# Second half of a hybrid diffusion layer: SyncE's transfers in written order, convolution blocks spread evenly, four output tiles

## The chip, the cores and the metric

The kernel runs on one core of a Trainium2 chip. The metric is the device time of one launch in microseconds (us), the median of several runs; lower is better.

A core has engines with an instruction stream each: TensorE (PE in the profile, with its weight loads as PEld), VectorE (DVE), ScalarE (ACT), GpSimd (POOL) and SyncE (SP). SyncE and ScalarE issue transfers between HBM and the on-chip memory SBUF; each issues them in the order of its own stream, so a transfer whose wait isn't over holds everything behind it on that engine. Matmul results go to PSUM, which has eight banks here.

## The reference

One layer of a backbone with two groups of heads. The context has 256 tokens, the latent grid 2048 tokens in 32 rows of 64. The input projection, shortened:

```python
def trunk_layer(x, mod, grid, h0, ...):
    h = rms_norm(x, g_pre) * (1 + scale) + shift
    u = h @ w_in
    z, xbc, dt_raw, ga, gb, gsil = jnp.split(u, ...)
    y_ssd, h_fin = ssd_branch(z, xbc, dt_raw, ...)
    y_conf = conformer_branch(ga, gb, ...)          # on the grid
    y_conf = y_conf.reshape(...) * jax.nn.silu(gsil)
    out = jnp.concatenate([y_ssd, y_conf], axis=-1) @ w_out
    return x + gate * rms_norm(out, g_post), h_fin

def conformer_branch(ga, gb, conv_w, conv_b, ln_g, ln_b):
    h = ga * jax.nn.sigmoid(gb)
    h = depthwise_conv(h, conv_w, conv_b)           # 31 taps down the columns
    return jax.nn.silu(layer_norm(h, ln_g, ln_b))
```

`ssd_branch` is a two-way Mamba-2 scan in chunks of 128 tokens: inside a chunk, products with a matrix of decays; between chunks, a state of 128 × 64 for each of 16 heads, forward and backward.

## The kernel before

The 2304 tokens (18 tiles of 128: two of context, sixteen of the latent grid) are worked in two halves, tiles 0 to 9 and 10 to 17. Within a half, the projection runs channel block by channel block: a unit takes a weight block of 1024 × 128, split into a high and a low part (wh, wl), and makes for each token block one PSUM group of 24 matmuls (lines 461 to 463). `gab_unit` makes two groups for a token block, gb and ga, gates them (line 625) and stores the result in GL[j] (line 626); `silu_unit` makes the z and gate blocks (store in line 639). wh and wl have three buffers each and are loaded by `load_w` (lines 418 and 419); a unit's load waits until the buffer of the unit three before it is free.

The stretch that the change touches is the second half behind its xbc blocks. There 21 units (eight of ga and gb, eight of z, five of the gate) make up `blocks`, a generator of steps of three matmuls, of which 392 are taken in this stretch. Between these steps run, as generators that are advanced a step at a time:

- the scan over tiles 9 to 17 (`scan`, `pass_a`), a new tile every seven steps. A tile loads xT and bc (lines 733 and 735), transposes them on TensorE (lines 778 and 855), loads rows of decays lb on ScalarE's queue (line 746), masks them on GpSimd (758), exponentiates them on ScalarE (766), mixes them on VectorE (770, 771), multiplies (802, 809, 815 to 817), copies the backward state out (sb, line 831, stored in 832) and sums the output tile yg (838 to 845, stored in 846). The tile yg starts with a skip term (838), which VectorE makes from xT.
- the convolution of the latent grid, eight blocks of 128 channels (`lat_conv`). A block loads kernels kd and image cx (`lat_load`, lines 698 and 699), copies the kernels into order (kt, 707), does 1024 small matmuls into four PSUM banks cp, two by two (718), evacuates each on VectorE into cvv (722), and stores cvv in four transfers (727). kd and cx have two buffers, kt and cvv one. A block asks for the next one's load when its GL is ready.
- the convolution of the context, four blocks on VectorE (`ctx_conv`), whose steps lie between the latent blocks.

PSUM has three banks "mm" for the projection and five banks "ss". A tile's px, pb, py, po and pst and a block's cp all come from the five.

What sets the order: a framework builds every engine's stream by a scheduler that uses its own estimates of durations, and keeps the dependences. An engine wrapped in the class `InOrder` keeps the written order while its flag `on` is set (line 81 is then the profile's line for what it issues). Before, the flag of SyncE is set at the start of the kernel and not here.

The loop of the stretch, before:

```python
extra = chain(f for j in range(4) for f in (lat(2 * j), ctx_conv(j + 4, cg), lat(2 * j + 1)))
sc_ = scan(range(9, NT))
run(take(blocks, 24))
interleave(take(blocks, 24), [sc_] * 4, 24)
interleave(take(blocks, 344), merge(sc_, 63, extra, 8 * 6 + 4 * 13), 344)
```

`merge` distributes the 100 steps of `extra` evenly among 63 of the scan.

Of the kernel before, what the change touches and what calls it, by code (L numbers as in the profile page):

```python
# [8 lines left out]
F32 = mybir.dt.float32  # L9
# [8 lines left out]
P = 128  # L18
# [30 lines left out]
def merge(a, na, b, nb):  # L49

    steps, x, y = [], 0, 0
    for _ in range(na + nb):
        if y * na >= x * nb and x < na or y >= nb:
            steps.append(a)
            x += 1
        else:
            steps.append(b)
            y += 1
    return steps


def take(gen, n):
    for _ in range(n):
        yield next(gen, None)
# [20 lines left out]
def backbone_kernel(ctx, tc, xa, xt_in, cols, rows, wconv, conf_b, gp_row, bg_row, state0, w_mod, w_dt, w_in, w_out,  # L85
# [3 lines left out]
    V, S, T, DMA = (InOrder(tc, e) for e in (nc.vector, nc.scalar, nc.tensor, nc.sync))  # L89
# [30 lines left out]
    def place(i):  # L120

        return (0, i) if i < HT[0] else (1, i - HT[0])
# [66 lines left out]
    pa = ph_a.enter_context(tc.tile_pool(name="pa", bufs=1))  # L189
# [423 lines left out]
    def gab_unit(half, j, hb):  # L613
        wb = next_w()
        wa = next_w()
        gl_done.discard(j)
        for b in ORDER[half]:
            BN, o = BNS[b], TOK[b]
            pg = bank("mm", f"gb{half}_{j}_{b}")
            yield from mm_cm(pg, wb, hb[b])  # L620
            th = ev(f"gth{half}_{j}_{b}")[:, :BN]
            S.activation(th, pg[:, :BN], AF.Tanh, scale=0.5)
            pa_ = bank("mm", f"ga{half}_{j}_{b}")
            yield from mm_cm(pa_, wa, hb[b])
            V.scalar_tensor_tensor(th, th, 1.0, pa_[:, :BN], ADD, MUL)
            DMA.dma_start(GL[j][:, o:o + BN], th)
        if half:
            gl_done.add(j)

    def silu_unit(half, c0, dst, j, hb, order=None):  # L630
        w = next_w()
        for b in order or ORDER[half]:
            BN, o = BNS[b], TOK[b] - half * HT[0] * P
            ps = bank("mm", f"sp{half}_{c0}_{j}_{b}")
            yield from mm_cm(ps, w, hb[b])
            th = ev(f"sth{half}_{c0}_{j}_{b}")[:, :BN]
            S.activation(th, ps[:, :BN], AF.Tanh, scale=0.5)  # L637
            V.scalar_tensor_tensor(th, th, 1.0, ps[:, :BN], ADD, MUL)  # L638
            DMA.dma_start(dst[half][j * P:(j + 1) * P, o:o + BN], th)


    def gate_rows():
        acc = [slab(f"gacc{a}") for a in range(2)]
        for k in range(KT):
            wg = big(f"wg{k}")
            DMA.dma_start(wg, w_mod[k * P:(k + 1) * P, 2 * D:3 * D])
            for a in range(2):
                if k == 0:
                    V.here("tensor_scalar", acc[a][:, :D], wg, sc[:, a, 0:1], None, MUL)
                else:  # L650
                    V.here("scalar_tensor_tensor", acc[a][:, :D], wg, sc[:, a, k:k + 1], acc[a][:, :D], MUL, ADD)
            yield
        br = [slab("bgr0")[0:1, :D], slab("bgr1")[0:1, :D]]
        DMA.dma_start(br[0], bg_row)
        DMA.dma_start(br[1], gp_row)
        for a in range(2):
            for n in range(2):
                ps = bank("ss", f"gp{a}{n}")
                cs = slice(n * 512, (n + 1) * 512)
                T.matmul(ps[0:1, :], ones[:, 0:1], acc[a][:, cs], start=True, stop=True)  # L660
                o = big(f"gr{a}{n}")[0:1, :512]
                V.tensor_tensor(o, ps[0:1, :], br[0][:, cs], ADD)
                V.tensor_tensor(o, o, br[1][:, cs], MUL)
                DMA.dma_start(GGD[a:a + 1, cs], o)
        yield


    def ctx_conv(j, tile):
        g = tile(f"cg{j}")
        G.memset(g[:, 0:15], 0.0)  # L670
        G.memset(g[:, 271:286], 0.0)
        DMA.dma_start(g[:, 15:271], GL[j][:, 0:256])
        yield
        acc = g[:, 512:768]
        w0 = C_CONFW + j * CW
        V.here("tensor_scalar", acc, g[:, 0:256], cv[:, w0:w0 + 1], cfb2[:, j:j + 1], MUL, ADD)
        for t in range(1, CW):
            V.here("scalar_tensor_tensor", acc, g[:, t:t + 256], cv[:, w0 + t:w0 + t + 1], acc, MUL, ADD)
            if t % 3 == 0:
                yield  # L680
        o = g[:, 768:1024]
        S.mul(o, acc, 0.5)
        DMA.dma_start(CV[j * P:(j + 1) * P, 0:256], o)
        yield
# [6 lines left out]
    def lat_load(j, lp):  # L691
        kd = lp.tile([P, 32, 32], F32, tag="kd", name=f"kd{j}", bufs=2)
        x = lp.tile([P, 32, 64], F32, tag="cx", name=f"cx{j}", bufs=2)
        lat_in[j] = kd, x
        for a in range(4):
            rs = slice(a * 32, (a + 1) * 32)
            src = bass.AP(tensor=wconv.tensor, offset=(j * 4 + a) * 64 * 32, ap=[[32, 32], [1, 1024]])
            DMA.dma_start(kd[rs].rearrange("p r g -> p (r g)"), src)
            DMA.dma_start(x[rs], GL[j][:, 256:].rearrange("(g a) (r w) -> a r g w", a=4, w=64)[a])

    def lat_conv(j, lp, cbb, more):
# [28 lines left out]
    def pass_a(i):  # L730
        half, il = place(i)
# [102 lines left out]
        yg = {}  # L834

        def skip(g):
            yg[g] = pa.tile([P, 4, P], F32, tag="yg", name=f"yg{i}{g}", bufs=2)
            V.tensor_tensor(yg[g], xT[:, 4 * g:4 * g + 4, :],
                            cv[:, C_D + 4 * g:C_D + 4 * g + 4].unsqueeze(2).to_broadcast([P, 4, P]), MUL)

# [77 lines left out]
    def scan(tiles):  # L918

        gens = [pass_a(i) for i in tiles]  # L920
        live, t = [], 0
        while gens or live:
            if gens and t % 7 == 0:
                live.append(gens.pop(0))
            for g in list(live):
                if next(g, 0) == 0:
                    live.remove(g)
            t += 1
            yield


    def interleave(blocks, side, n):
        done = 0
        total = len(side)
        for a, _ in enumerate(blocks):
            want = min(total, -(-total * (a + 1) // n))
            while done < want:
                next(side[done], None)
                done += 1
        while done < total:  # L940
            next(side[done], None)
            done += 1

    def chain(gens):
        for g in gens:
            yield from g

    def run(gen):
        for _ in gen:
            pass  # L950

    def post(half, nb):
        return chain([gab_unit(half, j, hb) for j in range(8)] + [silu_unit(half, Z0, ZS, j, hb) for j in range(8)]
                     + [silu_unit(half, GS0, GS, j, hb) for j in range(nb)])
# [76 lines left out]
    extra = chain([gate_rows()] + [ctx_conv(j, big) for j in range(4)])  # L1031
# [21 lines left out]
    lp = ph_l.enter_context(tc.tile_pool(name="lp", bufs=1, side="right"))  # L1053
# [4 lines left out]
    blocks = post(1, 5)  # L1058
    cg = lambda name: lp.tile([P, D], F32, tag="cg", name=name, bufs=2)
    lat = lambda j: lat_conv(j, lp, cbb, gl_done.__contains__)  # L1060
    extra = chain(f for j in range(4) for f in (lat(2 * j), ctx_conv(j + 4, cg), lat(2 * j + 1)))
    sc_ = scan(range(9, NT))
    run(take(blocks, 24))
    interleave(take(blocks, 24), [sc_] * 4, 24)
    interleave(take(blocks, 344), merge(sc_, 63, extra, 8 * 6 + 4 * 13), 344)
    run(sc_)
    run(extra)
    ph_l.close()
    ph_a.close()

# [105 lines left out]
    def norms(i, yz, nq):  # L1176

        pm = bank("ss", f"pm{i}")
        src = [(c, e, t[1]) for c, e, t in ((0, 4.0 * EPS, yz), (1, EPS, nq)) if t]
        for c, e, t in src:  # L1180
            T.matmul(pm[:, c:c + 1], t, ones[:, 0:1], start=True, stop=True)
        rs = []
        for c, e, t in src:
            ms = p1.tile([P, 1], F32, tag=f"ms{c}", name=f"yms{i}{c}", bufs=2)
            V.tensor_scalar(ms, pm[:, c:c + 1], 1.0 / D, e, MUL, ADD)
            rs.append((c, rstd_of(p1, ms, f"yr{i}{c}")))
        return rs
# [116 lines left out]
    i = order[0]  # L1304
# [21 lines left out]
    for b in range(2):  # L1326
        for m, u in enumerate(last):
            run(take(u, 8))
            if b == 0 and m == 1:
                rs = norms(i, yz, None)  # L1330
# [18 lines left out]
            if b == 1 and m == 0:  # L1349
                rs = norms(i, None, nq)  # L1350
                nq = conf_sqsum(i1, vv[1][0])
            if b == 1 and m == 1:
                n, v = nn[0], vv[0][0]
# [3 lines left out]
            if b == 1 and m == 2:  # L1357
                gs0, v0, n = gs_load(i), v, nn[1]
# [17 lines left out]
    i, nxt, nx2 = order[:3]  # L1376
    banks(i)
    out_part(pso[i], yh, 0, 1)
    rs = norms(nxt, yz, nq)
# [42 lines left out]
    n, n2 = n2, conf_load(order[3])  # L1422
    yh = yhn

    for a, i in enumerate(order[1:], 1):
# [7 lines left out]
        rs = None if last else norms(nxt, yz, nq)  # L1433
# [46 lines left out]
        if a + 3 < NT:  # L1480
            ssd_load(order[a + 3])
            n, n2 = n2, conf_load(order[a + 3])
        else:
            n = n2
# [72 lines left out]
```

## Time and profile before

| | us |
|---|---|
| median of three runs | 1852.8 |
| least, most | 1851.51, 1853.14 |
| the profiled execution, its own time | 1855.05 |
| its span, first to last instruction | 1853.3 |

The profile is one execution. Its busy times are shares of the span; a row of waits is read "engine, line, waits for", then the total in us, how often, and the longest. "SPq" is SyncE's queue as it issues a transfer. A row of windows holds a stretch, its length, the busy time (and instruction count) of each engine in it, the granted clock of TensorE as a part of full speed, and the transfers' share and rate. A time on a row of issues ("to landing") runs from the issue to the arrival of the data. The rows that matter are in the prediction.

### The profile page before, as it was taken

How to read it: one execution, taken by the hardware profiler on the slowest of the kernel's cores; microseconds unless marked ns; L12 is line 12 of the kernel's file. 1: busy time of each engine (PE TensorE's matmuls, PEld its weight loads, DVE VectorE, ACT ScalarE, POOL GpSimd, SP SyncE). 2: the span in 40 equal slices, each digit the busy share in tenths (PEclk: the TensorE clock that was granted, in tenths of full speed). 3: DMA queues.
4: the chain of work that ended last, by engine and by line, in shares of the span. 5: the costliest groups of instructions: out<-in, count | busy, mean ns of one | idle time of the engine just before them, and what ended most of it. 6: DMA issues, size and time to landing. Idle time of an engine off the chain costs nothing.

```text
span 1853.3 us, 29884 instructions
## 1 busy us (share of the span) xinstructions
PE 1793.9 (97%) x11167; PEld 1480.5 (80%) x11167; DVE 1216.5 (66%) x1847; ACT 867.1 (47%) x1960; POOL 172.2 (9%) x281
## 2 busy tenths in 40 slices
PE   5999999999999999999999889999999999999998
PEld 2888887888888888888877667777787888888886
DVE  4597857575666762687457375868347878777763
ACT  4747424444455431744235344554245545454441
POOL 1002001011111000100002011110000101111110
PEclk9999999999999999999999889999999999999999
DMA  9656566554786654545697889694977666656632
GB/s 334 215 198 238 204 212 212 190 201 162 261 267 216 222 182 145 178 170 201 195 207 225 176 239 233 229 236 176 290 223 238 194 184 167 172 171 170 185 103 80
DMA packets 304429, 375.22 MB, mean 202 GB/s; under 512 B 84246, under 2 KB 203670, under 8 KB 304284
## 3 DMA queue, kind: packets, MB, share of 16 engines
q1 hardware_dynamic: 283548, 335.56, 58.1%
q10 hardware_dynamic: 20736, 37.76, 7.3%
q8 instruction: 88, 1.44, 0.3%
q14 instruction: 57, 0.47, 0.1%
HBM read 243.66 MB, written 129.59 MB: 201 GB/s over the span
## 4 chain that ended last, share of the span: by engine, by line
PE 87%; DMA 8%; issue 1%; ACT 1%; DVE 1%; SPq 1%; POOL 0%; ACTq 0%; POOLq 0%; DVEq 0%
PE op L81 21%; PE sp L461 6%; PE sp L462 6%; PE sp L463 6%; PE xp L462 5%; PE xp L461 5%; PE xp L463 5%; PE ga L461 3%; PE ga L463 3%; PE ga L462 3%; PE gb L461 3%; PE gb L463 3%; PE gb L462 3%; DMA lb<-lt 3%; PE py L802 2%; PE po L809 2%
## 5 line engine op out<-in xcount | busy, mean ns | idle before, releaser
L766 ACT ACTIVATE lb<-lb,WB 128x128 f32<-128x128 f32 x576 | 184.5, 391 | 162.7 <-POOL lb L758 156.6
L461 PE MATMUL sp<-hh,wh 128*128 128x512 f32 (+1 forms) x640 | 240.0, 375 | 0.0
L463 PE MATMUL sp<-hh,wl 128*128 128x512 f32 (+1 forms) x640 | 237.1, 371 | 0.0
L462 PE MATMUL sp<-hl,wh 128*128 128x512 f32 (+1 forms) x640 | 237.0, 370 | 0.0
L758 POOL TENSOR_SCALAR_AFFINE_SELECT lb<-lb 128x512 f32<-128x512 f32 x144 | 109.1, 761 | 729.9 <-ACT el L755 400.5
L463 PE MATMUL xp<-hh,wl 128*128 128x512 f32 (+1 forms) x456 | 168.0, 368 | 0.0
L462 PE MATMUL xp<-hl,wh 128*128 128x512 f32 (+1 forms) x456 | 167.8, 368 | 0.0
L461 PE MATMUL xp<-hh,wh 128*128 128x512 f32 (+1 forms) x456 | 167.0, 367 | 0.0
L558 DVE SCALAR_TENSOR_TENSOR cva<-raw,cwh,cva 128x1280 f32<-128x1280 f32 (+1 forms) x96 | 141.9, 1487 | 20.4 <-ACT cva L552 18.2
L463 PEld LDWEIGHTS sp<-hh,wl 128*128 128x128 f32 x640 | 121.3, 189 | 21.1
L461 PEld LDWEIGHTS sp<-hh,wh 128*128 128x128 f32 x640 | 121.6, 190 | 20.7 <-issue 0.2
L462 PEld LDWEIGHTS sp<-hl,wh 128*128 128x128 f32 x640 | 121.6, 190 | 20.0
L461 PE MATMUL ga<-hh,wh 128*128 128x512 f32 (+1 forms) x320 | 121.3, 379 | 6.4 <-DMA wh<-whd 5.5
L75 DVE SCALAR_TENSOR_TENSOR cg<-cg,cv 128x256 f32<-128x256 f32 x240 | 123.0, 512 | 3.3
L461 PE MATMUL gb<-hh,wh 128*128 128x512 f32 (+1 forms) x320 | 120.5, 376 | 0.0
L463 PE MATMUL ga<-hh,wl 128*128 128x512 f32 (+1 forms) x320 | 119.2, 373 | 0.5 <-DMA wl<-wld 0.5
L462 PE MATMUL ga<-hl,wh 128*128 128x512 f32 (+1 forms) x320 | 119.4, 373 | 0.0
L463 PE MATMUL gb<-hh,wl 128*128 128x512 f32 (+1 forms) x320 | 119.0, 372 | 0.0
L462 PE MATMUL gb<-hl,wh 128*128 128x512 f32 (+1 forms) x320 | 118.9, 371 | 0.0
L770 DVE TENSOR_TENSOR lb<-lb,lb 128x512 f32<-128x512 f32 x72 | 50.8, 706 | 90.0 <-ACT lb L766 71.7
L638 DVE SCALAR_TENSOR_TENSOR sth<-sth,sp 128x512 f32<-128x512 f32 (+1 forms) x80 | 50.4, 630 | 75.6 <-ACT sth L637 70.7
L755 ACT ACTIVATE el<-lb 64x256 f32<-64x256 f32 x136 | 56.3, 414 | 88.8 <-DMA lb<-lt 71.2
(273 smaller groups left out, 3832.9 us busy)
## 6 DMA issues: line engine op xcount, KB each, us to landing
lb<-lt ACTq DMA_DIRECT2D x144, 256.0 KB, 4.6
wr<-in_w_in SPq DMA_DIRECT2D x88, 256.0 KB, 4.9
whd<-wh SPq DMA_DIRECT2D x44, 512.0 KB, 3.4
wld<-wl SPq DMA_DIRECT2D x44, 512.0 KB, 5.2
wh<-whd SPq DMA_DIRECT2D x44, 512.0 KB, 5.5
wl<-wld SPq DMA_DIRECT2D x44, 512.0 KB, 5.9
xT<-xb SPq DMA_DIRECT2D x18, 512.0 KB, 4.2
yp<-yg SPq DMA_DIRECT2D x36, 256.0 KB, 4.9
```

What stands on the lines that cost most here:

```text
L75: return self._tc.keep_in_program_order(getattr(self._eng, name)(*a, **k))
L81: return lambda *a, **k: self._tc.keep_in_program_order(f(*a, **k))
L461: T.matmul(ps[:, :BN], wh[:, k, :], hh[:, k, :], start=(k == 0), stop=False)
L462: T.matmul(ps[:, :BN], wh[:, k, :], hl[:, k, :], start=False, stop=False)
L463: T.matmul(ps[:, :BN], wl[:, k, :], hh[:, k, :], start=False, stop=(k == KT - 1))
L558: V.scalar_tensor_tensor(a[:, :n], raw[:, t:t + n], cwh[:, ct * 5 + t:ct * 5 + t + 1], a[:, :n], MUL, ADD)
L638: V.scalar_tensor_tensor(th, th, 1.0, ps[:, :BN], ADD, MUL)
L755: S.activation(el[g][rs, q:q + 2, :], E[g, hq, 0][rs, j::2, :], AF.Exp)
L758: G.affine_select(E[g, hq, d], E[g, hq, d], pattern=[[0, 4], [sg, P]], compare_op=ALU.is_ge, fill=NEG, base=0, channel_multiplier=-sg)
L766: S.activation(lb[:, h, :], lb[:, h, :], AF.Exp, bias=WB[:, i, c + h:c + h + 1])
L770: V.tensor_tensor(a, a, E[g, hq, 1], ADD)
L802: T.matmul(py[g][j * HD:(j + 1) * HD, q * P:(q + 1) * P], xt[g][:, h * HD:(h + 1) * HD], E[g, hq, 0][:, t, :], start=True, stop=True)
```

## The change

Four things change, all in the second half.

1. `lat_load` brings kd in one transfer of 128 × 1024 (512 KB), before four of 32 × 1024 (128 KB each). The four of cx stay.
2. The output tile yg has four buffers, in another pool, in the second half; before, two.
3. The convolutions: the first block's load is a step of its own at the start; then, for each j, seven steps of a context block, a latent block, the other six steps, a latent block. So the latent blocks are evenly spaced, and each asks for the next one's load early. `extra` has 101 steps.
4. SyncE keeps the written order for the stretch (`DMA.on = True`).

```diff
@@ -692,10 +692,10 @@
         kd = lp.tile([P, 32, 32], F32, tag="kd", name=f"kd{j}", bufs=2)
         x = lp.tile([P, 32, 64], F32, tag="cx", name=f"cx{j}", bufs=2)
         lat_in[j] = kd, x
+        src = bass.AP(tensor=wconv.tensor, offset=j * 4 * 64 * 32, ap=[[64 * 32, 4], [32, 32], [1, 1024]])
+        DMA.dma_start(kd.rearrange("p r g -> p (r g)"), src)
         for a in range(4):
             rs = slice(a * 32, (a + 1) * 32)
-            src = bass.AP(tensor=wconv.tensor, offset=(j * 4 + a) * 64 * 32, ap=[[32, 32], [1, 1024]])
-            DMA.dma_start(kd[rs].rearrange("p r g -> p (r g)"), src)
             DMA.dma_start(x[rs], GL[j][:, 256:].rearrange("(g a) (r w) -> a r g w", a=4, w=64)[a])
@@ -834,7 +834,8 @@
         def skip(g):
-            yg[g] = pa.tile([P, 4, P], F32, tag="yg", name=f"yg{i}{g}", bufs=2)
+            pool, n = (lp, 4) if half else (pa, 2)
+            yg[g] = pool.tile([P, 4, P], F32, tag="yg", name=f"yg{i}{g}", bufs=n)
@@ -948,6 +949,10 @@
+    def run_once(f):
+        f()
+        yield
@@ -1058,13 +1063,17 @@
     lat = lambda j: lat_conv(j, lp, cbb, gl_done.__contains__)
-    extra = chain(f for j in range(4) for f in (lat(2 * j), ctx_conv(j + 4, cg), lat(2 * j + 1)))
+    ctxs = [ctx_conv(j + 4, cg) for j in range(4)]
+    extra = chain([run_once(lambda: lat_load(0, lp))]
+                  + [f for j in range(4) for f in (take(ctxs[j], 7), lat(2 * j), take(ctxs[j], 6), lat(2 * j + 1))])
     sc_ = scan(range(9, NT))
+    DMA.on = True
     run(take(blocks, 24))
     interleave(take(blocks, 24), [sc_] * 4, 24)
-    interleave(take(blocks, 344), merge(sc_, 63, extra, 8 * 6 + 4 * 13), 344)
+    interleave(take(blocks, 344), merge(sc_, 63, extra, 1 + 8 * 6 + 4 * 13), 344)
     run(sc_)
     run(extra)
+    DMA.on = False
```

Two places in the order of the instructions show what moves. The first is on SyncE, around the weight wh3232, that of the ga block of the sixth channel block (names: kd and cx are the convolution's loads, cv its stores, yp and st the scan's stores, gl the gated results, bc and xT a tile's loads). Before:

```order
L698 DMA kd4_10488<-in_wconv 32x1024 x3
L699 DMA cx3_9706<-gl3_71 32x32x64 x4
L846 DMA yp11_90<-yg110_9630 128x512
L832 DMA st11_108<-sb110_9965 128x512
L626 DMA gl4_72<-gth1_4_3_9718 128x512
L698 DMA kd5_10795<-in_wconv 32x1024
L727 DMA cv_78<-cvv2_9760 32x32x64 x4
L698 DMA kd5_10795<-in_wconv 32x1024
L735 DMA bc13_10312<-xb1_64 128x4x128
L698 DMA kd5_10795<-in_wconv 32x1024 x2
L418 DMA wh3232_1_9646<-whd17_137 128x1024
L419 DMA wl3232_1_9645<-wld17_181 128x1024
```

Now:

```order
L81 DMA kd2_9438<-in_wconv 128x1x1024
L81 DMA cx2_9439<-gl2_70 32x32x64 x4
L81 DMA gl3_71<-gth1_3_4_9427 128x512
L81 DMA wh4256_1_9567<-whd25_145 128x1024
L81 DMA wl4256_1_9566<-wld25_189 128x1024
L81 DMA wh3232_1_9571<-whd17_137 128x1024
L81 DMA wl3232_1_9570<-wld17_181 128x1024
L81 DMA cv_78<-cvv1_9451 32x32x64 x4
L81 DMA cg5_9739<-gl5_73 128x256
L81 DMA xT12_9779<-xb1_64 128x8x128
L81 DMA bc12_9781<-xb1_64 128x4x128
L81 DMA gl4_72<-gth1_4_3_9693 128x512
```

The weight stood behind stores of the convolution and parts of kd4 and kd5, two blocks of the convolution ahead of their turn. It now stands directly behind the pair wh4256 and wl4256, and the tile loads xT12 and bc12 stand behind it, four stores and a context load.

The second place is on ScalarE, around the copy of tile 9's second backward state, sb91 (lb are rows of decays: L746 loads one, L766 exponentiates it; the first digits after lb are the tile). Before:

```order
L746 DMA lb10100_9051<-lt1_116 128x512
L766 ACTIVATE lb10010_8985<-lb10010_8985,WB_257 128x128 x4
L746 DMA lb11011_9392<-lt1_116 128x512
L746 DMA lb10110_9113<-lt1_116 128x512
L831 COPY sb91_9016<-pst911_8959 128x512
L864 CAST bth10_9022<-pb10_8967 128x256
L782 COPY xt100_9028<-px100_8972 128x512
L866 COPY cb10_9024<-pb10_8967 128x256
L755 ACTIVATE el101_8880<-lb10100_9051 64x256 x2
L792 CAST xwh1000_9086<-xw1000_9085 128x512
L766 ACTIVATE lb10100_9051<-lb10100_9051,WB_257 128x128 x4
L782 COPY xt101_9093<-px101_9038 128x512
```

Now:

```order
L746 DMA lb10110_9042<-lt1_116 128x512
L766 ACTIVATE lb11001_9314<-lb11001_9314,WB_257 128x128 x4
L766 ACTIVATE lb11011_9374<-lb11011_9374,WB_257 128x128 x2
L755 ACTIVATE el101_8754<-lb10110_9042 64x256 x2
L766 ACTIVATE lb11011_9374<-lb11011_9374,WB_257 128x128 x2
L746 DMA lb11101_9425<-lt1_116 128x512
L766 ACTIVATE lb10110_9042<-lb10110_9042,WB_257 128x128 x4
L766 ACTIVATE lb11101_9425<-lb11101_9425,WB_257 128x128 x4
L746 DMA lb11111_9554<-lt1_116 128x512
L622 ACTIVATE gth1_2_4_9046<-gb1_2_4_8881 128x512
L766 ACTIVATE lb11111_9554<-lb11111_9554,WB_257 128x128 x4
L831 COPY sb91_8888<-pst911_8834 128x512
```

The copy sb91 stood directly behind the loads of lb11011 and lb10110 and ahead of their exponentials. It now stands behind the exponentials of both and of lb11101 and lb11111, whose loads are issued between. The same holds for sb101, sb111 and sb131; each of the four frees the PSUM bank that the second matmul group of a convolution block takes next (blocks 0, 1, 2 and 4).

## The prediction

> **What bounds the kernel now.** I read the page's totals first, then a table by stage, then the waits of TensorE in the stretch that the change touches, then the chain of waits there. The totals say that TensorE is the bound: it is busy for nearly the whole span.
>
> ```profile
> span 1853.3 us, 29884 instructions
> ## 1 busy us (share of the span) xinstructions
> PE 1793.9 (97%) x11167; PEld 1480.5 (80%) x11167; DVE 1216.5 (66%) x1847; ACT 867.1 (47%) x1960; POOL 172.2 (9%) x281
> ```
>
> So the change can win only where TensorE (PE) stands still or runs slowly. The table by stage (length, then busy time and instruction count of PE, PEld, DVE, ACT and POOL, then the granted clock, the DMA share and GB/s) shows where that is: ahead of the scan, with the scan and the convolutions beside the weight groups, and behind them.
>
> ```profile
> 880.00:950.00 70.00, 69.49 (x569) 56.84 (x568) 33.55 (x41) 20.03 (x29) 1.09 (x5) 1.00 0.72 192
> 950.00:1300.00 350.00, 324.12 (x3314) 255.56 (x3314) 237.61 (x408) 165.65 (x415) 44.84 (x63) 0.95 0.80 216
> 1300.00:1420.00 120.00, 118.12 (x570) 98.31 (x567) 59.75 (x82) 47.73 (x89) 2.69 (x4) 1.00 0.81 258
> ```
>
> From 950 to 1300 us PE is idle for 350 − 324.12 = 25.9 us, and the clock is 0.95 where it is 1.00 on either side. That is the whole field of this change. PE's waits between 950 and 1420 us name the 25.9 us almost completely (columns: total, times, longest):
>
> ```profile
> PE ga L461 <- DMA wh<-whd: 5.5, 1, 5.5
> PE px L778 <- issue: 5.3, 2, 4.1
> PE cp L718 <- DVE cvv L722: 4.4, 1, 4.4
> PE pst L815 <- DVE cvv L722: 3.5, 1, 3.5
> PE cp L718 <- issue: 2.6, 1, 2.6
> PE pst L815 <- ACT xwh L792: 1.7, 1, 1.7
> PE cp L718 <- ACT sb L831: 1.4, 1, 1.4
> ...
> PE ga L463 <- DMA wl<-wld: 0.5, 1, 0.5
> ```
>
> These eight sum to 24.9 us. Three kinds matter: a weight that came late (5.5 + 0.5), the PSUM banks of the latent convolution that other engines had not emptied (4.4, 3.5, 2.6 and 1.4), and a tile's transposes that could not start (5.3).
>
> **The change part by part.** *The late weight: −6.0 us.* The chain of waits shows its origin: SyncE's queue (SPq) works through the stores of cvv (L727) and the parts of kd (L698) before it gets to the weight.
>
> ```profile
> 1054.16 0.56 SPq L727
> 1054.78 2.80 SPq L727
> 1057.62 1.51 SPq L727
> 1059.17 1.82 SPq L698
> 1061.52 0.50 SPq L698
> 1063.04 9.06 DMA wl<-wld
> ```
>
> The waits of SPq and the issues of kd say how long the queue had stood there, and what a kd part costs to issue (least, median and most, in ns):
>
> ```profile
> SPq L698 <- ACT kt L707: 24.2, 2, 14.7
> ```
>
> ```profile
> L698 SPq DMA_DIRECT2D kd<-in_wconv x32: 311/421/3385, 910.6 to 1159.7; - x32
> ```
>
> A kd part waits until the copy kt of two blocks before has freed its buffer, and wh3232 and wl3232 stand behind four such parts. In the changed order these two stand directly behind wh4256 and wl4256, and no kd is between. So both stalls of ga go, 5.5 + 0.5 = 6.0 us. The merge of four kd parts into one takes 32 − 8 = 24 issues off SPq, 24 × 0.421 = 10.1 us of queue over 350; apart from the stall just counted, no wait of PE names kd, so I give it nothing more (bounds: none to the 6.0 again, if the order alone had not been enough).
>
> *The blocks spread evenly: −5.8 us of old stalls.* cvv has one buffer. Blocks 1 and 2 of the convolution lie close together in the trace, and the 4.4 us come where the evacuation of block 2 waits for block 1's stores. Blocks one output channel tile apart have time for that, so 4.4 goes; so does the 1.4, whose place no longer exists. Bound: they stay, 0.
>
> *The banks, new stalls: +15.6 us.* This is the dearest term and the least certain. A block takes four of five "ss" banks, and a bank is free when the scan's use of it is evacuated. In the changed order blocks 0, 1, 2 and 4 get their second bank from a state copy sb (L831) on ScalarE, and that copy stands behind the exponentials of about three decay rows lb more than before. What a decay row costs is in the trace: mask, one exponential, and what ended POOL's and DVE's idle time ahead of lb.
>
> ```profile
> L758 POOL TENSOR_SCALAR_AFFINE_SELECT lb<-lb x59: 632/637/1806, 952.4 to 1272.7; 128x512 f32<-128x512 f32 x59
> L766 ACT ACTIVATE lb<-lb,WB x236: 377/387/406, 953.1 to 1274.7; 128x128 f32<-128x128 f32 x118
> ...
>   DMA lb<-lt: 149.5, 38
> ```
>
> A row is 4 × 0.387 = 1.5 us of ScalarE when its data is there, and an engine that waited for one stood 149.5 / 38 = 3.9 us. The sb copy used to be ahead of three such waits. Least is the 1.4 us that the trace shows for PE behind sb; most is three whole waits, 11.8 us. I take one wait, 3.9 us, since the two conv stalls that come from other evacuations (4.4 and 3.5) are of that size: 4 × 3.9 = 15.6. Bounds: 4 × 1.4 = 5.6 to 4 × 11.8 = 47.2, of which the upper would need PE to arrive early at all four.
>
> *The evacuations on VectorE: +3.5 us.* In blocks 5 and 6 the first bank is emptied by VectorE behind the mixing of lb16000 and lb17000. I price each by the 3.5 us of the row "pst <- cvv"; one such stall is there already, so the net is 3.5. Bounds 0 and 2 × 4.4 − 3.5 = 5.3.
>
> *The tile loads: +4.1 us.* In written order xT12 and bc12 stand behind wh3232 and wl3232, four stores of cvv1 and the load of cg5; each of these waits for somebody, and what is queued behind bc12 is the next gated result and the stores of tile 11. The transposes of tile 12 are what waits. The price is the longer wait of the row "px <- issue", 4.1 us, once. Bounds: 0, if the load was asked for early enough, and eight tiles at 4.1 (the second rival). The first weights of the stage, wh3744 and wl3744, now stand behind three stores of xb1 and four loads of cbb; PE shows no wait there in the trace, so I take 0, with 5.5 (the longest weight wait) as the other end.
>
> *yg with four buffers: 0.* VectorE's waits show what it removes:
>
> ```profile
> DVE yg L838 <- DMA yp<-yg: 10.6, 4, 4.2
> ```
>
> None of PE's rows names yg; the mix and the evacuation of cvv, which do stand behind it on VectorE, waited last for decay rows. Bounds: −3.5 (the "pst <- cvv" row, if the 4.2 us ahead of it had been its cause) to 0. The cover is that late decay row; were it early, the four buffers would be worth the 3.5.
>
> *The clock: +3.6 us.* Slices of 10 us in and behind stalls show what a stop costs afterwards:
>
> ```profile
> 1060.00:1070.00 10.00, 5.03 (x23) 3.81 (x21) 5.40 (x11) 4.82 (x12) 0.64 (x1) 0.91 0.91 241
> 1070.00:1080.00 10.00, 9.04 (x39) 6.75 (x40) 6.37 (x13) 4.61 (x12) 1.27 (x2) 0.75 0.82 280
> ...
> 1220.00:1230.00 10.00, 10.00 (x248) 7.75 (x250) 5.80 (x10) 4.40 (x13) 0.75 (x2) 1.00 1.04 292
> 1230.00:1240.00 10.00, 7.40 (x92) 5.86 (x79) 7.85 (x12) 8.81 (x22) 2.93 (x4) 0.66 0.65 201
> ```
>
> The slice at 1220 is full of the convolution's small matmuls at clock 1.00, so it is the stops that lower it. In the stage the loss is (1 − 0.95) × 324.12 = 16.2 us for 25.9 idle, 0.63 for each. The net idle of the terms above is −6.0 − 5.8 + 15.6 + 3.5 + 4.1 = +11.4; the clock adds at most 0.63 × 11.4 = 7.2 and at least 0. I take half, 3.6, because shorter stops need not be followed by a slow stretch.
>
> [...]
>
> *Sum.* 11.4 + 3.6 = +15.0 us on the profiled execution, whose time is its span of 1853.3 and 1.75 us around it, 1855.05: 1870. That execution stands 2.25 us (0.12%) above the median of the three runs, 1852.8, so the time forecast for the median is 1868 us, 0.8% slower. (A difference under 0.2%, 3.7 us, is about what a measurement of this kernel can't tell from none.)
>
> **The rivals.**
>
> *The old stalls go and nothing comes.* For it: the two named causes, a weight behind kd and cvv's one buffer, are in the rows, and both are removed; loads a block ahead have time to spare. Against it: the sb copies do stand later, and the banks were short already. Time: 1852.8 − 6.0 − 4.4 = 1842.4, and with the 1.4 and half the clock's 0.63 as low as 1837; if a part of the bank stalls comes, 1844 to 1849. It decides if PE reaches the second banks more than 3.9 us after the scan's last use.
>
> *SyncE's written order holds the tile loads in every tile.* One mechanism: a store that waits for VectorE or ScalarE holds the next tile's xT and bc, and PE's transposes wait. Each of eight tiles (10 to 17) pays the 4.1, against 5.3 in all now: 32.8 − 5.3 = 27.5 in place of the 4.1, so +23.4 more than the forecast, about 1891. It decides from the point where the queue stands longer than the pass leaves between a load's turn and its use; the 14.7 us of the row above show that SPq can stand so long. Weights would suffer last: two units of two groups of 24 matmuls at 118.12 / 570 = 0.207 us are 20 us ahead. [...]
>
> *Gain and loss cancel.* If each sb copy costs the 1.4 us that the trace shows, the banks are 5.6 in place of 15.6, and the net idle is +1.4: 1854. That is within 0.2%.
>
> **How the numbers follow.** The forecast 0.57, the late tile loads 0.13, the cancelling 0.10, the faster rival 0.20. The forecast's own range is from sb at 2.0 us a copy (4 × 1.9 = 7.6 less idle, 3.8 and 1.2 of clock: 1858) to sb at 6.0, half of the 11.8 (4 × 2.1 = 8.4 more, 19.8 idle and 0.63 for each: 1885). The range to hold the time 8 times in 10 is 1844 to 1884: it leaves out the lower part of the faster rival and the upper part of the late loads. Faster by over 0.2%: 0.20; within 0.2%: 0.10; slower: 0.57 + 0.13 = 0.70.
>
> **What would show it.** In the changed profile: no wait of ga on wh or wl near 3232 (if there is one, the −6.0 is wrong); PE's waits of cp on sb in blocks 0, 1, 2 and 4, some 4 us each (if they are absent, the +15.6 is, and the time is below 1855); a wait of px near tile 12 that ends with SPq; the stage from the first conv block to the last longer than 350 us with PE idle near 37; its clock below 0.95. SPq's wait for the copy kt should be gone. The prediction is wrong if the idle time of PE in that stage falls below 25.9 us.

## The result, and the profile after

The changed kernel takes 1912.3 us (median of 4 runs, 1910.7 to 1916.5) where the kernel before takes 1852.2 in the same comparison: ratio 1.0314, interval 1.0294 to 1.0335. It is slower by some 60 us, four times the forecast of 15, and outside the range. Totals of the page, changed kernel:

```profile
span 1911.3 us, 29862 instructions
## 1 busy us (share of the span) xinstructions
PE 1808.6 (95%) x11167; PEld 1492.2 (78%) x11167; DVE 1214.9 (64%) x1847; ACT 866.8 (45%) x1960; POOL 171.3 (9%) x281
```

The span is 58.0 us longer; TensorE (PE) works 14.7 us longer on the same 11167 matmuls (mean granted clock 0.975, before 0.987) and is idle 43.3 us more. The table by stage, with the middle stage now some 60 us longer (to 1360 us):

```profile
880.00:950.00 70.00, 70.00 (x331) 57.58 (x330) 33.29 (x37) 14.53 (x20) 0.24 (x4) 1.00 0.48 152
950.00:1360.00 410.00, 344.99 (x3473) 272.57 (x3473) 241.62 (x417) 172.57 (x425) 45.11 (x64) 0.90 0.75 194
1360.00:1480.00 120.00, 117.52 (x682) 97.98 (x679) 60.34 (x82) 48.53 (x90) 2.69 (x4) 1.00 0.84 265
```

PE is idle for 410 − 345.0 = 65.0 us in the stage (before 25.9; the prediction had about 37), and the clock is 0.90 in place of 0.95. Of the 43.3 us of added idle time, 39.1 lie in the stage that the change touches; the rest is spread outside it. PE's longest waits there (the columns as before: total, times, longest):

```profile
PE pb L854 <- DMA bc<-xb: 10.4, 3, 6.3
PE cp L718 <- issue: 9.5, 3, 4.7
PE cp L718 <- ACT sb L831: 7.9, 2, 4.6
PE pst L815 <- ACT xwh L792: 7.4, 3, 6.1
PE po L809 <- DVE cvv L722: 6.6, 1, 6.6
PE pst L815 <- DVE yo L823: 5.9, 2, 3.2
PE ga L461 <- ACT gth L622: 4.3, 2, 4.0
PE pst L815 <- ACT sb L831: 4.2, 1, 4.2
PE cp L718 <- DVE yg L844: 2.8, 1, 2.8
PE py L802 <- DVE lb L771: 2.4, 1, 2.4
```

No row has ga waiting for a weight: that first term came true. But there is no one dear wait either. Everything is late by a little, which suggests that the cause lies further up. It shows in kd. In a window around the third block of the convolution, the load is issued at 1038.2 us, and the copy kt that waits for it starts at 1051.1:

```profile
L81 SPq DMA_DIRECT2D kd<-in_wconv x1: 557/557/557, 1038.2 to 1038.2; - x1
L707 ACT COPY kt<-kd x1: 1997/1997/1997, 1051.1 to 1051.1; 128x1024 f32<-128x1024 f32 x1
its engine sat idle before it (us, times) until:
  DMA kd<-in_wconv: 5.8, 1
```

That is 12.9 us for 512 KB, from the issue to the copy. Before, four parts of 128 KB were issued within 2.7 us and landed after 4.1 us (median; rows of kd between 1127 and 1134 us, kernel before; over all 32 parts the least, median and most were 2.5, 5.0 and 7.5):

```profile
L698 SPq DMA_DIRECT2D kd<-in_wconv x4: 419/421/1731, 1127.8 to 1130.5; - x4
...
DMA to landing us min/median/max: 3.8/4.1/4.4
```

The last two columns of a table of windows of 1 us (the share of the 16 DMA engines that was busy, and GB/s) show why. Changed kernel, the end of that load:

```profile
1048.00:1049.00 1.00, 1.00 (x11) 0.59 (x9) 1.00 (x2) 0.00 (x0) 0.00 (x0) 1.00 0.24 66
1049.00:1050.00 1.00, 1.00 (x8) 0.74 (x5) 0.75 (x2) 0.00 (x0) 0.00 (x0) 1.00 0.23 61
```

With a share of 0.24 the sixteen engines together do the work of about four (0.24 × 16 = 3.8, an estimate), at 61 to 66 GB/s. What stands behind it in the queue lands late too. In the changed kernel the four parts of the image cx are issued directly behind kd. Their time from issue to landing (least, median, most), there and in the kernel before:

```profile
DMA to landing us min/median/max: 6.5/13.6/15.8
```

```profile
DMA to landing us min/median/max: 3.9/6.4/10.7
```

The chain of waits shows how far that reaches (changed kernel, from the load of the first part of the fifth block's image cx, which stands behind that block's kd; pieces in order of time, start and length):

```profile
1146.18 14.94 DMA cx<-gl
...
1161.14 0.02 ACTq L746
...
1161.20 5.31 DMA lb<-lt
...
1172.70 0.64 POOL lb L758
```

ScalarE's own queue (ACTq) issued the load of the decay row at 1161.20, when cx of SyncE's queue had landed at 1161.12. No data goes from one to the other; in the trace both count their completion on the same semaphore, number 102, and the wait ahead of the issue on ScalarE, at 1161.14, is for it. ScalarE stood still for it:

```profile
ACT kt L707 <- DMA cx<-gl: 11.2, 1, 11.2
```

The row was masked at 1172.7, 26.5 us after cx had been issued. This is one path from a slow kd to waits of other kinds on PE.

### The profile page after: what moved, and what is told of

The parts are those of the page before. It is cut to its first block, busy times and chain, and to the rows that moved or that the text cites. A ratio compares the mean times of both kernels' runs of the same rounds, so it can differ in the third digit from the quotient of the medians.

```text
span 1911.3 us, 29862 instructions
## 1 busy us (share of the span) xinstructions
PE 1808.6 (95%) x11167; PEld 1492.2 (78%) x11167; DVE 1214.9 (64%) x1847; ACT 866.8 (45%) x1960; POOL 171.3 (9%) x281
## 5 line engine op out<-in xcount | busy, mean ns | idle before, releaser
L766 ACT ACTIVATE lb<-lb,WB 128x128 f32<-128x128 f32 x576 | 184.9, 391 | 184.8 <-POOL lb L758 156.1
L461 PEld LDWEIGHTS xp<-hh,wh 128*128 128x128 f32 x456 | 86.0, 189 | 14.2
L462 PEld LDWEIGHTS xp<-hl,wh 128*128 128x128 f32 x456 | 86.0, 189 | 14.1
```

Of the source, the lines that this page charges most:

```text
L461: T.matmul(ps[:, :BN], wh[:, k, :], hh[:, k, :], start=(k == 0), stop=False)
L462: T.matmul(ps[:, :BN], wh[:, k, :], hl[:, k, :], start=False, stop=False)
L766: S.activation(lb[:, h, :], lb[:, h, :], AF.Exp, bias=WB[:, i, c + h:c + h + 1])
```

## The experiments

Two theories after the result. **K**: kd in one transfer keeps only about four DMA engines busy (the share of 0.24), and its lateness spreads. **O**: the written order on SyncE alone, as the prediction had it, only larger. All ratios are to the kernel before in the same comparison.

**Kd in four parts again** (the rest of the change stays).

```diff
-        src = bass.AP(tensor=wconv.tensor, offset=j * 4 * 64 * 32, ap=[[64 * 32, 4], [32, 32], [1, 1024]])
-        DMA.dma_start(kd.rearrange("p r g -> p (r g)"), src)
         for a in range(4):
             rs = slice(a * 32, (a + 1) * 32)
+            src = bass.AP(tensor=wconv.tensor, offset=(j * 4 + a) * 64 * 32, ap=[[32, 32], [1, 1024]])
+            DMA.dma_start(kd[rs].rearrange("p r g -> p (r g)"), src)
```

> The changed kernel, with kd loaded in four transfers of 32x1024 again; written order, even blocks and four yg stay. Theory K (the one transfer of kd runs on four of the sixteen DMA engines, takes 10 to 16 us from issue to landing in place of 4 to 7, and holds up what is queued behind it on SyncE and, through shared completion counters, on ScalarE's queue): most of the 60 us go, 1855 to 1885. Theory O (the written order of SyncE alone is the cause, as the prediction had it, only larger): 1895 to 1915.

Measured: 1.0128 (1.0111 to 1.0145), 1882.2 us beside 1858.5. Some 36 of the 60 us go with this edit; 23.6 us stay. Both theories hold a part. The median landing of cx is 7.9 us here. PE's waits of this run:

```profile
PE pb L854 <- DMA bc<-xb: 10.2, 4, 3.2
PE cp L718 <- issue: 8.7, 2, 4.7
PE po L809 <- DVE cvv L722: 6.4, 1, 6.4
...
PE cp L718 <- ACT sb L831: 0.2, 1, 0.2
```

PE's wait of cp for sb is 0.2 us here, where it was 7.9, though the copies sb stand as late among the exponentials on ScalarE as in the changed kernel.

**Kd in one transfer as the only change.** The same two lines, the other way, in the kernel before.

> The kernel before, with kd in one transfer as the only change. K: the landing of kd is 10 to 16 us here too and what stands behind it is late; slower, 1860 to 1890. O: the scheduler's order stays, 24 issues fewer on SyncE; 1845 to 1855.

Measured: 1.0184 (1.0158 to 1.0210), 1893.4 us, a little above what K expected: 35 us slower by this edit alone. With the 23.6 that the rest costs, the sum is 58.5, about the 60 of the whole change.

**Kd in two transfers, each with a slowest source dimension of 2.**

```diff
-        src = bass.AP(tensor=wconv.tensor, offset=j * 4 * 64 * 32, ap=[[64 * 32, 4], [32, 32], [1, 1024]])
-        DMA.dma_start(kd.rearrange("p r g -> p (r g)"), src)
+        for b in range(2):
+            src = bass.AP(tensor=wconv.tensor, offset=(j * 4 + 2 * b) * 64 * 32, ap=[[64 * 32, 2], [32, 32], [1, 1024]])
+            DMA.dma_start(kd[b * 64:(b + 1) * 64].rearrange("p r g -> p (r g)"), src)
```

> The changed kernel, with kd in two transfers whose slowest source dimension is 2 (two row blocks of 32 each) in place of one whose slowest is 4. K: each transfer runs on two engines, the pair lands after 20 us or more, and the time rises by another 8 x 5 to 8 x 10 us: 1950 to 1990. O: as the changed kernel, 1905 to 1918; if only size counted (256 KB each in place of 512 KB), a little below 1912.

Measured: 1.0434 (1.0410 to 1.0457), 1939.6 us, slower than the changed kernel's 1.0314 though each transfer is smaller. Windows of 1 us of this run, between the first issue of kd, at 938.7 us, and the copy kt that waited for kd until 956.2:

```profile
946.00:947.00 1.00, 1.00 (x6) 0.82 (x5) 0.45 (x1) 0.00 (x0) 0.00 (x0) 1.00 0.11 35
947.00:948.00 1.00, 1.00 (x6) 0.83 (x5) 0.00 (x0) 0.00 (x0) 0.00 (x0) 1.00 0.13 49
```

A share of 0.11 to 0.13 is the work of about two engines (0.12 × 16 = 1.9, an estimate). So it isn't the size of a transfer alone that decides: with a slowest source dimension of 4 the share was 0.24, with 2 it was 0.11 to 0.13. The time rose by some 22 us (1.0434 − 1.0314) and not by the 40 and more that were expected. A later kd may be partly hidden by what is late already; that was not tested.

**The changed kernel without the written order** (kd in one transfer stays; the two lines with `DMA.on` go).

> The changed kernel without the written order on SyncE (kd in one transfer, even blocks and four yg stay). K: still slower than before by 15 us or more, 1870 to 1905, since kd lands late whatever the order. O: back to 1845 to 1862.

Measured: 1.0172 (1.0144 to 1.0201). As K has it: kd in one transfer costs without the order too, and the written order adds 26 us on top (1.0314 − 1.0172, of 1855).

**What of the rest, 23.6 us, is the order, and what the even blocks?** Two kernels, both with kd in four parts: the written order as the only change, and the even blocks with four yg without the order.

> The kernel before, with the written order on SyncE in this stretch as the only change (kd in four parts, old spacing of the blocks, two yg). If the 23.6 us that are left without the merged kd come from the written order (theory W): 1.010 to 1.020 of before. If they come from the even blocks and the state copies sb that stand later on ScalarE (theory B, the prediction's dearest term): 0.998 to 1.004.

> The kernel before with the even blocks and the four yg, without the written order and with kd in four parts. W: 0.996 to 1.004 of before. B: 1.008 to 1.015.

Measured: the order alone 1.0218 (1.0202 to 1.0234); even blocks and yg 0.9979 (0.9965 to 0.9992). So the order is the loss, and the even blocks without it are no loss at all. The order costs 40 us with the old spacing, more than was expected, and 28 with the new one (1.0128 − 0.9979); against the kernel before, 24 of these 28 are seen, since the even blocks and the four yg gain 4. Without the order PE's longest wait is for the evacuation cvv, longer than the 4.4 of the kernel before, and no ga waits for a weight:

```profile
PE cp L718 <- DVE cvv L722: 12.0, 3, 7.3
```

This run doesn't test the prediction's dearest term, the copies sb behind the decay rows: without the written order ScalarE's order is another one as well, and the second sb of tile 9 stands directly behind the load of a row again, as in the kernel before.

PE's two longest waits with the order alone, and SyncE's longest:

```profile
PE cp L718 <- ACT kt L707: 33.0, 3, 14.3
PE cp L718 <- issue: 9.1, 3, 3.9
```

```profile
SPq L81 <- ACT cg L682: 69.7, 3, 27.4
```

With the old spacing a block is asked for just ahead of its use, and in written order kd can't pass what stands at the head of the queue. That is foremost the store of the context convolution (cg), which waits for ScalarE; how much of the 40 us is its doing was not tested.

**The even blocks alone** (two yg).

> The kernel before with the even blocks alone (two yg). If the even blocks carry the 0.9979 of the run with both: 0.996 to 1.000. If the four yg carry it (VectorE waited 10.6 us for stores of yg): 1.000 to 1.008.

Measured: 0.9996 (0.9982 to 1.0011). The interval overlaps that of the run with four yg; how the 0.2% divides isn't settled.

**A tile's bc asked for four steps earlier** (kd in four parts, order and even blocks stay).

```diff
             if gens and t % 7 == 0:
                 live.append(gens.pop(0))
+                todo.pop(0)
+            if DMA.on and todo and t % 7 == 3:
+                bc_load(todo[0])
```

> The changed kernel with kd in four parts, and with a tile's bc (line 735) asked for four steps of the scan earlier, still in written order; nothing else moves in the text. TensorE waited 10.2 us in four places for bc there. If the written order costs by late tile loads: the wait of pb for bc goes, 6 to 14 us less than with four parts alone, 1.005 to 1.010 of before. If those waits only cover others (decay rows, banks) that are late anyway: within 4 us of it, 1.011 to 1.015.

Measured: 1.0130 (1.0111 to 1.0150), no gain over 1.0128. PE's waits of this run (line numbers are 7 higher from the scan on):

```profile
PE po L816 <- DVE cvv L722: 12.3, 3, 8.3
PE cp L718 <- ACT sb L838: 7.5, 2, 4.5
PE px L785 <- DMA xT<-xb: 4.1, 3, 2.4
PE cp L718 <- DVE yg L851: 3.9, 1, 3.9
```

The 10.2 us of pb are gone, and others stand in their place, 12.3 for the evacuation first of all, and 7.5 of cp for sb, while the kernel takes the same time. As far as this run shows, the late tile load was a wait that covered others and not a cost; that the earlier bc delays other transfers by as much isn't excluded.

**Kd issued by ScalarE, in the kernel before.**

```diff
-            DMA.dma_start(kd[rs].rearrange("p r g -> p (r g)"), src)
+            S.dma_start(kd[rs].rearrange("p r g -> p (r g)"), src)
```

> The kernel before, with the four parts of kd issued by ScalarE in place of SyncE. The prediction's first term says that wh3232 and wl3232 are late only since parts of kd stand ahead of them on SyncE: the 6.0 us of TensorE's wait go and the time is 0.995 to 0.998 of before. If the 32 issues on ScalarE (0.33 us each) delay decay rows by as much: 0.999 to 1.004.

Measured: 0.9964 (0.9950 to 0.9979), 6.4 us faster. PE's longest wait for a weight in this run:

```profile
PE ga L461 <- DMA wh<-whd: 1.1, 1, 1.1
```

5.5 became 1.1: the prediction's first term, tested on its own. By its interval the gain is 4 to 9 us; this wait is 4.4 of it, and the clock of the stage rose to 0.96.

**The ga weight written where its buffer comes free** (kd in four parts, order and even blocks stay). In the run with four parts, SyncE's queue stood first of all for these weights:

```profile
SPq L81 <- PE gb L463: 62.3, 6, 15.6
SPq L81 <- DVE sth L638: 50.4, 11, 10.5
```

```diff
-        wa = next_w()
+        late = DMA.on and half
+        wa = wq.pop(0) if late else next_w()
...
             S.activation(th, pg[:, :BN], AF.Tanh, scale=0.5)
+            if late and b == ORDER[half][-1]:
+                wq.append(load_w(*wcols.pop(0)))
```

> The changed kernel with kd in four parts, and with the ga weight of the next unit written where its buffer comes free (behind the last gb group of a unit) in place of ahead of that unit. In the run with four parts SyncE's queue stood 62.3 us in six waits for the last gb group, with tile loads, kd, cx and stores behind. If this head of the queue is what the written order costs: those waits go, 12 us or more less than with four parts alone, 1.000 to 1.007 of before. If the other waits at the head (stores behind VectorE, shared counters) cost as much without it: within 5 us of it, 1.010 to 1.015.

Measured: 1.0071 (1.0046 to 1.0097), at the edge of the first expectation, and less than the 12 us that it named. SyncE's waits of this run:

```profile
SPq L81 <- DVE sth L641: 62.7, 11, 13.6
SPq L81 <- DVE gth L628: 54.9, 11, 9.1
```

The wait for gb is gone from the head of the list and with it 0.0057, 10 to 11 of the 24 us. Stores of gated results (gth), which the earlier list doesn't have, now wait there in its place. Thirteen us stay.

**Where the thirteen lie.** Three kernels take one group of transfers each out of the written order, and one control takes the whole order away. The edit is `nc.sync.dma_start` in place of `DMA.dma_start` for the group, or, in the control, no `DMA.on` in the stretch and `late = half == 1`.

> The run with the ga weights written later (1.0071 of before), with the scan's own four kinds of transfer (xT, bc, st, yp) taken out of the written order; weights, gated results and the convolution's transfers stay in it. If tile loads and tile stores that stand behind other heads of the queue are what the written order still costs: 0.996 to 1.002. If the rest lies in the convolution's transfers, the gated results or the even blocks with this order: 1.004 to 1.010.

> The run with the ga weights written later, with the convolutions' transfers (kd, cx, cv, cg) taken out of the written order; weights, gated results and the scan's transfers stay in it. TensorE waited 13.5 us there for the evacuation cvv. If late loads and stores of the convolution are what the written order still costs: 0.996 to 1.002 of before. If not: 1.004 to 1.010.

> The same run, with the stores of the gated results (lines 626 and 639 of before) taken out of the written order in place of the convolution's. SyncE stood 62.7 + 54.9 us for them. If a store that waits for VectorE at the head of the queue is what still costs: 0.996 to 1.002. If not: 1.004 to 1.010.

> A control: the same run without any written order (kd in four parts, even blocks, four yg, ga weights written later). If the written order is the whole of the 0.0071 that are left: 0.996 to 1.001. If writing the weights later costs by itself: 1.002 to 1.008.

Measured: the scan's transfers free 1.0076 (1.0056 to 1.0095); the convolutions' free 1.0059 (1.0039 to 1.0079); the results' stores free 1.0100 (1.0073 to 1.0128); no order 0.9979 (0.9963 to 0.9996). The control returns to the run of the even blocks: the thirteen are the order's, which costs 17 us here (1.0071 − 0.9979). But none of the three groups carries them: 1.0059 isn't clear of 1.0071, and the other two are no faster. The weights, a fourth group, were not taken out. Which of the order's waits they are stays open; that a late transfer holds a decay row through a shared semaphore, as cx did in the changed kernel (number 102, 11.2 us), would fit, and was not tried.

**What beats both.** The even blocks and four yg, kd in four parts issued by ScalarE, no written order.

> The kernel before with the even blocks and the four yg, and with the four parts of kd issued by ScalarE; no written order. If the two gains add up (0.9979 and 0.9964): 0.993 to 0.996. If they are the same stall counted twice: 0.996 to 0.999.

Measured: 0.9920 (0.9902 to 0.9938), 1839.2 us. The two gains add up (0.9979 × 0.9964 = 0.9943); that it is a little more than their sum isn't clear of the noise of the three runs. Its stage, and PE's longest waits there:

```profile
950.00:1300.00 350.00, 336.29 (x3655) 266.74 (x3654) 236.99 (x406) 170.95 (x422) 44.35 (x63) 0.98 0.82 225
```

```profile
PE cp L718 <- DVE cvv L722: 5.6, 1, 5.6
PE px L778 <- DVE cvv L722: 4.9, 1, 4.9
```

Idle is 13.7 us in place of 25.9 and the clock 0.98 in place of 0.95: with the stops, some of the clock's loss went too, (1 − 0.98) × 336.3 = 6.7 us where it was 16.2.

## Why the prediction was wrong, and where it was right

The sign held; the size did not, and the largest piece came from an edit that had been priced at nothing.

- **The late weight, −6.0.** Right: no such wait of ga is left after the change, and moving kd off SyncE by itself gave 6.4 us (4 to 9 by its interval), with 4.4 less of this wait. That the totals 6.0 and 6.4 lie so close is in part luck.
- **The old stalls of the blocks, −5.8.** Not shown. No row of cp for cvv is left in the changed kernel, but with the even blocks and no order it is 12.0 us where it was 4.4: spreading the blocks doesn't by itself give VectorE and the stores of cvv the time that the prediction counted on.
- **Merging kd, "nothing more" (bounds: none to a gain).** This is the step that failed first of all. The edit was costed only as 24 issues fewer on SyncE; its bound from the other side, a loss, was left out without a reason. It costs 35 us alone. No row of the trace before shows a transfer of that shape, so the rows could not have priced it; its DMA share of 0.24, and the 0.11 to 0.13 of the two smaller ones, were seen only in the runs.
- **The banks behind sb, +15.6.** Not confirmed as a cost. The changed kernel does show cp, pst and px waiting for sb, 7.9 + 4.2 + 1.0 us, near the price and so a tempting confirmation. But with kd in four parts cp's wait for sb is 0.2 us in one run and 7.5 in another (bc earlier), and both take the same time, 1.0128 and 1.0130 of before. So the wait comes and goes with what else is late and doesn't set the time there. How much of the order's cost passes through sb in the changed kernel stays open. That sb stands later in ScalarE's stream was read from an order, and an order has no time in it.
- **The evacuations, +3.5, and the tile loads, +4.1.** For the first, cp waits once for VectorE (yg), 2.8 us; the 6.6 of po for cvv is a wait that the prediction didn't have. For the second, it is pb that waits for bc, 10.4 us, and not px for xT. That one was tested: when it is taken away nothing is gained.
- **The clock, +3.6.** Too small with the rest: (1 − 0.90) × 345.0 = 34.5 us of loss for 65.0 idle, 0.53 for each, beside 0.63 before. The added 39.1 us of idle came with 18.3 of added loss, 0.47 for each, where the prediction took half of 0.63. The larger miss is the idle time that it was applied to.
- **The written order.** This is the second step that failed: the sum gave the order 4.1 us of late tile loads, and it costs 28 us with the even blocks and 40 alone. The prediction knew the mechanism as a rival at 0.13 and named the wrong heads: it argued that weights suffer last, as what waits. They are what makes others wait. A ga weight stands in the queue for a buffer that comes free only after the last gb group, up to 15.6 us at a time, and holds what is behind it; 10 to 11 us went when it was written later. The rest is shown to be the order's, and not which wait of it.
- **The faster rival.** The kernel could have been made faster: even blocks and four yg without the order give 0.9979, and with kd on ScalarE's queue 0.9920. The change joined the even blocks and the four yg, worth 4 us, to two edits that cost 35 and 28.

## What to carry to other kernels

Before several transfers become one, measure one of the new shape: here a slowest source dimension of 4 went with a DMA share of 0.24 and one of 2 with 0.11 to 0.13, and both cost time (1.0314 and 1.0434, where four parts took 1.0128). In a profile, windows of 1 us while such a load is in flight show that share. A written order on a queue that other engines wait for was only as good here as the latest item at its head, for which SyncE stood up to 15.6 us at a time with four parts; write a transfer where its buffer comes free, not where its use is planned (1.0128 became 1.0071). When one late thing makes every wait a little longer, price the waits only after the late thing has been found: taking one of them away, as with bc here, tells more about whether it is a cost or a cover than its length does.

## What the hardware showed that was not expected

For one transfer of 512 KB with a slowest source dimension of four, 12.9 us went by from the issue to the copy that waited for it; towards its end the DMA share was 0.23 to 0.24, at 61 to 66 GB/s. Two of 256 KB with a slowest source dimension of two showed a share of 0.11 to 0.13, at 35 to 49 GB/s. Four parts of 128 KB had landed after 5.0 us each (median of 32). The issue of a transfer on ScalarE's queue waited until one of SyncE's had landed, 14.9 us after that one's issue; both count on semaphore 102, and ScalarE stood 11.2 us for it.
